# One stage of a two-layer backbone: its instructions recorded, then issued in the order of a list scheduler in the kernel

## The chip, the cores and the metric

The kernel runs on one core of one Trainium2 chip. The metric is the device time of one execution in microseconds (us), lower is better. The core's engines each run their own queue in order: TensorE (PE, with its weight loads shown apart as PEld), VectorE (DVE), ScalarE (ACT), GpSimd (POOL) and SyncE (SP, which here only issues DMAs). POOL's queue issues DMAs too.

## The reference

Two layers over 256 context tokens and 512 latent tokens of width 1024. What matters here is the RWKV-7 time mixing of layer 0, with 8 heads of 64 in both directions (d = 0 and 1), and the modulation vectors of all layers:

```python
def step(S, inp):
    r_t, w_t, k_t, v_t, a_t, b_t = inp
    sa = jnp.einsum('bhij,bhj->bhi', S, a_t)
    S = (S * w_t[:, :, None, :] + sa[..., None] * b_t[:, :, None, :]
         + v_t[..., None] * k_t[:, :, None, :])
    return S, jnp.einsum('bhij,bhj->bhi', S, r_t)
s_fin, ys = lax.scan(step, state0, xs, reverse=reverse)
...
def ada_mods(cvec, w, b):
    m = jax.nn.silu(cvec) @ w + b
```

After the scan come a norm per head, a bonus term and a gate (`rwkv_out`). Beside time mixing, layer 0 has latent attention (MLA); then an output projection, a mixture of experts, and layer 1 with grouped-query attention and its own mixture.

## The kernel before

The stages run one after the other: `front` (input projections), time mixing (`rwkv`, run from `program`), `mla`, `outproj`, `moe`, `gqa`, `outproj`, `moe`. The change touches time mixing.

**Time mixing.** The sequence is cut into 6 windows `w` of 128 tokens, each of two chunks `ci` of 64; both directions go through it together. Per window and direction `prep` makes decays and scaled keys (matmuls `psw`, `psa`, `psb`; tiles AR and BK). Per chunk `units` makes products of keys (`psB`, `psK`), transposes BK (`psT`) and writes the triangular matrix Ad to DRAM (`adr`). `tload` and `tinv` read it back in another layout (`Ts`), invert its 16x16 blocks on DVE and send them through DRAM again (`tdr`) to the tiles TP and TQ: four DMAs in a row that follow each other. `tmat` makes the whole inverse `T` from TP and TQ by a chain that goes to and fro between PE (`psG`, three `psX`) and DVE or ACT. `chain` carries the state: `cX`, `cU`, `cS` (the next state) and `cY` (the output). `rwout` is `rwkv_out` for one window; three of the six run inside the stage, the others in `mla`.

**Beside it** `ada_steps` makes the modulation vectors: 80 loads of 512 KB (`adaw`, from POOL, into two buffers), each with four matmuls into `psa`, then per 16 loads a sum on DVE (`adar`), four transposes (`pta`), a copy to `fm` and a DMA `rows<-adar`. The loads are issued two ahead, so load i+2 is asked for when the matmuls of load i are done.

**What sets the order.** Python generators merge the threads (`merge`). The Tile scheduler then issues everything in the order of its own simulated timeline, by priority. `urgent` raises the priority of `chain` (UC) and `tmat` (UT), and `tc.issue_after(last())` holds each group of `adaw` matmuls behind the last matmul of the chain traced so far (`K['at']`). All of `mla` is in the same scheduler.

Of the kernel before, what the change touches and what calls it, by code (L numbers as in the profile page):

```python
# [6 lines left out]
F32=mybir.dt.float32; F32R=mybir.dt.float32r; I32=mybir.dt.int32  # L7
AF=mybir.ActivationFunctionType; ALU=mybir.AluOpType
PSUM=bass.MemoryType.PSUM; DRAM=bass.MemoryType.DRAM
UC=2500; UT=2000; UE=3000; FI={9:(0,1),10:(3,)}; TL=((2,),(4,5))  # L10
CDEC=float(np.exp(np.float64(-0.5)))

def vw(ap, dims, off=0):

    return bass.AP(tensor=ap.tensor, offset=ap.offset+off, ap=[list(ap.ap[0])]+[list(d) for d in dims])

MAGIC=0x5f3759df
# [16 lines left out]
def rwkv(tc, nc, K, y, bon, sa):  # L34
# [29 lines left out]
    def prep(w,d):  # L64
        sp=sa; pre=U_.setdefault(w,[])
# [3 lines left out]
        r,k,kk=rkk[:,0],rkk[:,1],rkk[:,2]  # L69
        T4=lambda nm,tag=None: sp.tile([128,2,4,64],F32,tag=tag or nm,name=nm,bufs=1)  # L70

        sgw=sp.tile([128,2,4,65],F32,tag="sg",name="sg",bufs=1); sg=vw(sgw,[[261,2],[65,4],[1,64]]); nc.gpsimd.memset(vw(sgw,[[196,2],[65,4]],64),0.0)
        a=T4("a"); lora=((K['w2'],K['tw1'],K['w0h'],sg,d,big("psw")),(K['a2'],K['a1'],K['a0h'],a,1-d,big("psa")))
# [126 lines left out]
    def chain(w,ci):  # L200
# [5 lines left out]
        for d in range(2): mm(psX[:,d],lambda h,hp: pre[d][1][:,cs[d],h,hp,:],lambda h,hp: su[:,d,h,0,hp,:])  # L206
        K['at']=last[0]
        X=sp.tile([128,2,4,64],F32,name="X",bufs=1); nc.scalar.copy(X,psX)
        yield
        psU=chm("cU")  # L210
        for d in range(2): mm(psU[:,d],lambda h,hp: T[:,d,hp,h,:],lambda h,hp: X[:,d,hp,:])
        K['at']=last[0]
        for h,hs in enumerate(HS): nc.scalar.copy(su[hs,:,h,1],psU[hs])
# [14 lines left out]
        for h,hs in enumerate(HS):  # L228

            for i in range(8): d,hp=divmod(i,4); nc.tensor.matmul(psY[hs,d,hp,:],lhsT=su[hs,d,h,0,hp,:],rhs=pre[d][1][hs,cs[d],2,hp,:],start=i==0,stop=False,skip_group_check=True)  # L230
            for i in range(8): d,hp=divmod(i,4); hy=nc.tensor.matmul(psY[hs,d,hp,:],lhsT=su[:,d,h,1,hp,:],rhs=rb[:,d,h,hp,:],start=False,stop=True,skip_group_check=True)
            K['at']=hy.ins
        for d in range(2): addy(psY[:,d],win(w,d)*2+cs[d])
        if w+1<W: vload(w+1,ci)
        yield
    def steps(j):
        w,ci=divmod(j,2)
        u=units(w,ci)
        if ci==0:
# [43 lines left out]
    def then(*gs):  # L283
        for g in gs: yield from g
    def urgent(g,n):

        while True:
            with tc.high_priority(offset=n): x=next(g,g)
            if x is g: return
            yield  # L290
    def thread():
        N=2*W
        vload(0,0); vload(0,1)
        yield from merge(urgent(tmat(0,0),UT),steps(2))
        for j in range(N):
            g=[urgent(chain(*divmod(j,2)),UC)]
            if j+1<N: g.append(urgent(then(*([tinv(j//2+1)] if j%2 else []),tmat(*divmod(j+1,2))),UT))
            if j+3<N: g.append(steps(j+3))
            if j in FI: g.append(outs(FI[j],spare))
            yield from merge(*g[::-1])  # L300
# [1014 lines left out]
def program(tc,D,out):  # L1315
    nc=tc.nc
    with tc.tile_pool(reuse_waits="tile",name="g",bufs=1) as gp, tc.tile_pool(reuse_waits="tile",name="dr",bufs=1,space=DRAM) as dp:
# [13 lines left out]
        c=K.c; RW=[]; pd,dp2=pool("rwd",space=DRAM)  # L1331
        def early(psum):
# [4 lines left out]
            for o,n,m in ((0,'bones',128),(128,'hsel',32)): nc.vector.tensor_scalar(bo[:,o:o+m],c[n],1.0/64,None,op0=ALU.mult)  # L1337
            pa,sa=pool("rwa","right")
            ph=sa.tile([128,24],F32,name="ph")
# [74 lines left out]
```

## Time and profile before

| | |
|---|---|
| median of 3 runs | 1866.99 us (1865.08 to 1882.0) |
| the profiled execution's own time | 1878.29 us |
| its span, first to last instruction | 1876.6 us |
| mean granted TensorE clock (1.00 is 2.4 GHz) | 0.922 |
| busy: PE, DVE, ACT, POOL | 1600.1, 1252.2, 891.6, 481.5 us |
| time mixing, from 255 to 657 us of the span | 402 us: PE busy 312.0, DVE 226.9, ACT 133.8 |

Busy times are summed by the profiler from the instructions it saw; idle time is put down to the event that ended it (the releaser). An engine that is idle costs time only where it lies on the path to the end, so the stage is read by the waits on its busiest engine.

### The profile page before, as it was taken

The page shows a single profiled execution, that of the slowest core. Times are in us where ns is not written, and L with a number is a line of the kernel's source. Part 1 is how long each engine was busy: PE and PEld are TensorE (multiplying, and loading weights), DVE is VectorE, ACT ScalarE, POOL GpSimd, SP SyncE. Part 2 cuts the span into 40 slices and gives each one's busy share as a digit, 9 for nine tenths or more (in the row PEclk, how much of TensorE's full clock was granted, in tenths as well). Part 3 has the DMA queues.
Part 4 walks back from the last instruction along what each step waited for, and adds up shares of the span by engine and source line. Part 5 has one row for each costly group of instructions (what it writes and reads, how often), then busy time and mean ns, then how long its engine had stood idle before and what let it go on. Part 6 is the DMA issues. An engine that isn't in the chain of part 4 may idle for free.

```text
span 1876.6 us, 31790 instructions
## 1 busy us (share of the span) xinstructions
PE 1600.1 (85%) x12258; PEld 1225.2 (65%) x12258; DVE 1252.2 (67%) x2306; ACT 891.6 (48%) x1734; POOL 481.5 (26%) x512
## 2 busy tenths in 40 slices
PE   4999968777788787899986999969969999779986
PEld 2888856555576675566864877757746667457765
DVE  3575666555555586554487978777975553889986
ACT  5432644333332263665233867526356663447651
POOL 0222011111111032000244776063500001524324
PEclk8999879888789897899988999989989999889998
DMA  9245456676755220101646999752020004469974
GB/s 357 67 115 138 115 153 174 198 211 172 208 164 143 53 97 24 45 1 54 207 157 205 362 364 322 266 170 75 14 65 23 1 12 159 161 229 366 359 291 168
DMA packets 179002, 303.39 MB, mean 162 GB/s; under 512 B 93968, under 2 KB 107152, under 8 KB 177824
## 3 DMA queue, kind: packets, MB, share of 16 engines
q1 hardware_dynamic: 142576, 189.61, 30.3%
q0 software_dynamic: 29984, 101.27, 16.3%
q10 hardware_dynamic: 6288, 10.45, 1.8%
q8 instruction: 97, 1.59, 0.3%
q14 instruction: 57, 0.47, 0.1%
HBM read 266.99 MB, written 42.15 MB: 165 GB/s over the span
## 4 chain that ended last, share of the span: by engine, by line
PE 51%; DVE 18%; DMA 14%; issue 10%; ACT 4%; POOL 2%; SPq 1%; ACTq 0%; POOLq 0%; DVEq 0%
PE ps L959 7%; PE ps L510 6%; DMA adaw<-in_ada_w 6%; PE sc L650 4%; PE pt L664 4%; PE pv L672 4%; PE py L959 3%; PE py L836 3%; PE ps L836 3%; DMA w<-in_w_ex 3%; PE psq L595 3%; DVE wl L401 3%; PE ps L1240 1%; PE psX L42 1%; PE psa L452 1%
## 5 line engine op out<-in xcount | busy, mean ns | idle before, releaser
L401 DVE TENSOR_TENSOR wl<-w,wh 128x1024 fp32r<-128x1024 f32 (+2 forms) x214 | 281.5, 1338 | 64.8 <-ACT wh L400 53.2
L400 ACT CAST wh<-w 128x1024 fp32r<-128x1024 f32 (+2 forms) x241 | 246.9, 1048 | 131.1 <-PE ps L959 30.9
L959 PE MATMUL ps<-wh,xTl 128*128 128x512 f32 x336 | 136.9, 408 | 10.8 <-DVE xTl L401 9.4
L959 PE MATMUL ps<-wh,xTh 128*128 128x512 f32 x336 | 136.7, 407 | 3.9 <-ACT xTh L400 3.9
L959 PE MATMUL ps<-wl,xTh 128*128 128x512 f32 x336 | 133.7, 398 | 0.0
L651 DVE TENSOR_REDUCE nm<-sc 128x1 f32<-128x768 f32 (+1 forms) x112 | 96.5, 879 | 53.5 <-PE sc L650 52.7
L664 PE MATMUL pt<-cst,p 128*128 128x128 f32 x608 | 107.7, 291 | 11.3 <-ACT pT L666 6.5
L653 ACT ACTIVATE p<-sc,nm 128x768 f32<-128x768 f32 (+1 forms) x112 | 94.0, 842 | 44.6 <-DVE nm L651 44.6
L443 POOL DMA_DIRECT2D adaw<-in_ada_w x80 | 42.4, 532 | 274.2 <-PE psa L452 262.6
L664 PEld LDWEIGHTS pt<-cst,p 128*128 128x128 f32 x608 | 68.6, 143 | 56.5 <-issue 33.8
L672 PE MATMUL pv<-pT,vv 128*64 128x256 f32 x608 | 101.3, 413 | 1.1 <-ACT pT L666 0.6
L452 PE MATMUL psa<-adaw,sct 128*32 128x256 f32 x640 | 62.7, 459 | 40.2 <-DMA adaw<-in_ada_w 37.5
L1142 POOL DMA_INDIRECT w<-in_w_ex,wat x72 | 87.3, 1213 | 35.9 <-DVE wl L401 18.2
L401 POOL TENSOR_TENSOR wl<-w,wh 128x1024 fp32r<-128x1024 f32 x27 | 69.5, 2593 | 84.6 <-ACT wh L400 84.5
L510 PE MATMUL ps<-hhi,wh 128*128 128x512 f32 (+1 forms) x240 | 81.1, 346 | 5.0 <-DVE hhi L400 5.0
L959 PEld LDWEIGHTS ps<-wh,xTl 128*128 128x128 f32 x336 | 64.3, 191 | 29.5 <-DVE xTl L401 15.1
L510 PE MATMUL ps<-hlo,wh 128*128 128x512 f32 (+1 forms) x240 | 81.9, 342 | 0.0
L510 PE MATMUL ps<-hhi,wl 128*128 128x512 f32 (+1 forms) x240 | 81.8, 343 | 0.0
L666 ACT COPY pT<-pt 128x512 f32<-128x512 f32 x104 | 60.2, 586 | 44.5 <-PE pt L664 43.9
L959 PEld LDWEIGHTS ps<-wh,xTh 128*128 128x128 f32 x336 | 64.7, 193 | 17.1 <-ACT xTh L400 5.8
L401 DVE TENSOR_TENSOR xTl<-pt,xTh 128x512 fp32r<-128x512 f32 x84 | 55.8, 681 | 27.1 <-ACT xTh L400 26.1
L959 PEld LDWEIGHTS ps<-wl,xTh 128*128 128x128 f32 x336 | 64.6, 192 | 12.9
(611 smaller groups left out, 4321.0 us busy)
## 6 DMA issues: line engine op xcount, KB each, us to landing
w<-in_w_ex SPq DMA_DIRECT2D x120, 512.0 KB
adaw<-in_ada_w POOLq DMA_DIRECT2D x80, 512.0 KB
Yd<-yb SPq DMA_DIRECT2D x35, 512.0 KB
w<-in_w_sh SPq DMA_DIRECT2D x24, 512.0 KB
rkk<-rkk SPq DMA_DIRECT2D x12, 768.0 KB
adaw<-in_ada_w SPq DMA_DIRECT2D x8, 1024.0 KB
w<-in_w_rw SPq DMA_DIRECT2D x15, 512.0 KB
SU<-Vd SPq DMA_DIRECT2D x48, 128.0 KB
```

The costliest lines, as they stand in the source:

```text
L400: e1(hi,src)
L401: return e2(lo,src,hi.bitcast(F32),ALU.subtract)
L452: nc.tensor.matmul(ps[32*c:32*c+32,256*h:256*h+256],lhsT=K.sc[:,k,:],rhs=w[:,256*c:256*c+256],start=k+h==0,stop=k==7,skip_group_check=True ...
L510: nc.tensor.matmul(ps[:,:n],lhsT=a[:,k,:],rhs=b[:,k,sl],start=k+j==0,stop=k==7 and j==2)
L650: for m,(a,b) in enumerate(pl): nc.tensor.matmul(ps[:,c0:c0+cn],lhsT=a,rhs=b[:,c0:c0+cn],start=m==0,stop=m==len(pl)-1)
L651: nm=sp.tile([128,1],F32,name="nm",bufs=8); i1=nc.vector.tensor_reduce(nm,ps[:,:n],X,ALU.max,negate=True)
L653: K.late=i1,nc.scalar.activation(p[:,:n],ps[:,:n],AF.Exp,bias=nm,accum_out=rs[:,j:j+1])
L664: for j in range(nq): nc.tensor.transpose(pt[:,y,128*j:128*j+128],PR[y][0][j][:,128*kt:128*kt+128],K.ident)
L672: nc.tensor.matmul(po[64*y:64*y+64,:w],lhsT=v(h+y,kt),rhs=T[:,y],start=kt==0,stop=kt==nk-1,skip_group_check=True)
L836: nc.tensor.matmul(ps,lhsT=a[:,128*i:128*i+128],rhs=b[:,k%2,:],start=j==0,stop=j==23); j+=1
L959: for n,(x,y) in enumerate(((a[0],b[0]),(a[0],b[1]),(a[1],b[0]))): nc.tensor.matmul(ps,lhsT=x,rhs=y,start=first and n==0,stop=last and n==2)
L1142: return lambda t,j: nc.gpsimd.indirect_dma_start(out=t,out_offset=None,in_=D['w_ex'],in_offset=bass.IndirectOffsetOnAxis(ap=ix[:,j:j+1],a ...
```

## The change

`program` wraps the builder `nc` in a class `Plan`. Between `nc.start()` and `nc.stop()`, that is for all of time mixing's main part and `ada_steps`, instructions are recorded and not issued (`keep`), with the areas that they read and write and so what each depends on; tiles that take a buffer over depend on its former users. `stop` puts PE instructions of one kind and one merge step (`SEG`) into groups, prices every instruction from a table (`cost`; a DMA lands 2.2 us and its bytes' time after its issue, one DMA's bytes at a time, `wire`), finds for each group the longest way to the end (`bl`), and runs a list scheduler with those prices: a free engine takes the ready group with the longest way. The groups are then issued in that order in a `manual_schedule` block. The priorities (`urgent`) of the main part and `issue_after` for the `adaw` matmuls are gone, and a small memset in `prep` (`sg`) goes from POOL to DVE. No other instruction is added or taken away. `front`, with the first steps of time mixing, and `mla` are scheduled as before.

```diff
-UC=2500; UT=2000; UE=3000; FI={9:(0,1),10:(3,)}; TL=((2,),(4,5))
+UE=3000; FI={9:(0,1),10:(3,)}; TL=((2,),(4,5))
...
+    def cost(self,o):
+        e,n,m=o['eng'],o['n'],o['m']
+        if m=='dma_start': return 0.06 if e=='sync' else 1.0
+        if e=='tensor':
+            if m=='transpose': return 0.109 if n>=128 else 0.07
+            k=o['sh'][0]; c=0.072 if n<=64 else n*0.00168
+            if o['p']==32: return c*0.4
...
+        if e=='scalar': return 0.22+n*0.00076
+        return 0.9+n*0.002
+    def wire(self,o):
...
+        return b/(3.4e5 if row>=2048 else 2.4e5 if row>=1024 else 1e5)
...
+    def stop(self):
+        self.on=False; ops=self.ops; N=len(ops)
...
+        lat=[(2.2+self.wire(ops[g[0]])) if dma[k] else t[k]+(0.1 if eng[k]=='tensor' else 0)+SEM for k,g in enumerate(G)]
...
+        for k in reversed(order): bl[k]=lat[k]+max((bl[s] for s in succ[k]),default=0.0)
...
+            for e in self.ENG:
+                while free[e]<=now and ready[e]:
+                    _,k=heapq.heappop(ready[e]); done+=1; out.append(k); at[k]=now
+                    free[e]=now+t[k]; heapq.heappush(wake,free[e])
+                    if dma[k]:
+                        b=self.wire(ops[G[k][0]]); dfree=max(dfree,now)+b; end=dfree+2.2
+                    else: end=now+lat[k]
+                    heapq.heappush(fut,(end,k))
...
+        with self.tc.manual_schedule():
+            for k in out:
+                for i in G[k]: o=ops[i]; o['f'](*o['a'],**o['k'])
...
-nc.gpsimd.memset(vw(sgw,[[196,2],[65,4]],64),0.0)
+nc.vector.memset(vw(sgw,[[196,2],[65,4]],64),0.0)
...
-            g=[urgent(chain(*divmod(j,2)),UC)]
-            if j+1<N: g.append(urgent(then(*([tinv(j//2+1)] if j%2 else []),tmat(*divmod(j+1,2))),UT))
+            g=[chain(*divmod(j,2))]
+            if j+1<N: g.append(then(*([tinv(j//2+1)] if j%2 else []),tmat(*divmod(j+1,2))))
...
+    nc=Plan(tc,tc.nc)
...
-            main,tail=body(sp,pp)
-            run_all(merge((ada_steps(nc,tc,K,[(0,1),(0,2),(1,0),(1,1),(1,2)],D,sp,pp,lambda: Q.get('at')),1),(main,PM)))
+            sp,pp=nc.pool(sp),nc.pool(pp); main,tail=body(sp,pp); nc.start()
+            run_all(merge((ada_steps(nc,tc,K,[(0,1),(0,2),(1,0),(1,1),(1,2)],D,sp,pp,lambda: None),1),(main,PM)))
+            nc.stop()
```

The order moves on every engine. In the rows below, L172 is the line of the change that issues the recorded instructions, L26 the wrapper's line for all others; `x4` counts equal instructions.

**Place 1: PE, early in the stage.** Before, from the first direction matmuls of a `prep` to the state matmuls of the first chunk:

```order
L75 MATMUL psw<-tw_96,w_98 128x128 x4
L452 MATMUL psa<-adaw,sct 32x256 x4
L75 MATMUL psa<-a_97,a_99 128x128 x4
L42 MATMUL cU<-X,T_2314 64x64
L452 MATMUL psa<-adaw,sct 32x256 x4
L42 MATMUL cU<-X,T_2314 64x64 x15
L42 MATMUL psG<-TQ_1578,Aoff 64x64 x16
L452 MATMUL psa<-adaw,sct 32x256 x4
```

The change, PE, from the end of a `prep`'s matmuls past the `cX` of the second chunk:

```order
L172 MATMUL psw<-tw_96,w_98 128x128
L172 MATMUL psa<-a_97,a_99 128x128
L172 MATMUL cX<-SU,AR_1622 64x64 x8
L172 MATMUL cX<-SU,AR_1807 64x64 x8
L172 MATMUL psa<-adaw,sct 32x256 x4
L172 MATMUL psX<-Aoff,L_2313 64x64 x16
L172 MATMUL psa<-adaw,sct 32x256 x4
L172 MATMUL psb<-q,hs 32x128 x4
```

Matmuls of one kind are no longer cut into, `psw` and `psa` of a `prep` always alternate, and loads of `adaw` are spread over the whole stage.

**Place 2: DVE, from the end of a `tinv` (`Ts<-tmp`) to the transpose that needs what came back through DRAM (TP and TQ).** Before, third window:

```order
L170 TENSOR_REDUCE Ts_1913<-tmp_2254 128x8x8
L467 TENSOR_SCALAR A_8910<-fm_85 128x16
L468 TENSOR_TENSOR A_8910<-A_8910,par 128x16
L108 TENSOR_TENSOR bon<-psb,bon 128x128
L124 TENSOR_TENSOR AR_1807<-psB,cst 64x256
L125 TENSOR_TENSOR Rb_2368<-psB,cst 128x256
L124 TENSOR_TENSOR AR_1807<-psK,cst 64x256
L125 TENSOR_TENSOR Rb_2368<-psK,cst 128x256
L184 STREAM_TRANSPOSE TP_1568<-TQ_1576 128x256
```

The change, the same window:

```order
L172 TENSOR_TENSOR kd<-kd,rkk 128x512
L172 TENSOR_TENSOR BK_1808<-bb,En 128x8x64
L172 SCALAR_TENSOR_TENSOR AR_1807<-rkk,E_2521 64x2x256 x2
L172 TENSOR_TENSOR AR_1807<-rkk,E_2521 128x2x256
L172 TENSOR_TENSOR BK_1808<-kd,En 128x8x64
L172 TENSOR_TENSOR q<-rkk,kd 128x512
L172 TENSOR_TENSOR Aoff<-Ad_1669,cst 128x512 x2
L172 TENSOR_TENSOR SU<-cS,Dw 64x256 x2
L172 TENSOR_TENSOR AR_1807<-psB,cst 64x256
L172 TENSOR_TENSOR Rb_2330<-psB,cst 128x256
L172 TENSOR_TENSOR AR_1807<-psK,cst 64x256
L172 TENSOR_TENSOR Rb_2330<-psK,cst 128x256
```

Right ahead of these rows stands `Ts<-tmp`, right behind them `bon<-psb,bon` and the transpose: the instructions of a whole `prep` now stand in the time of the way through DRAM.

**Place 3: PE and SP, the end of the stage.** PE before, from the last `cU` on; `ro`, `pt` and `pq` belong to `mla`:

```order
L42 MATMUL cU<-X,T_2315 64x64 x15
L231 MATMUL cY<-Rb_2581,SU 64x64 x8
L230 MATMUL cY<-AR_2764,SU 64x64 x4
L230 MATMUL cY<-AR_3109,SU 64x64 x4
L231 MATMUL cY<-Rb_2581,SU 64x64 x8
L256 MATMUL ro<-y,bo_1522 128x512
L736 MATMUL pt<-cst,p 128x128 x5
```

PE in the change, the same place:

```order
L172 MATMUL cU<-X,T_2315 64x64 x16
L172 MATMUL psa<-adaw,sct 32x256 x4
L172 MATMUL rg<-sgw,roc 128x128 x4
L172 MATMUL psa<-adaw,sct 32x256 x4
L172 MATMUL cY<-Rb_2366,SU 64x64 x16
L172 MATMUL psa<-adaw,sct 32x256 x40
L172 MATMUL pta<-cst,adar 128x128 x4
L26 MATMUL ro<-y,bo_1522 128x512
L26 MATMUL pt<-cst,p 128x128 x5
```

SP in the change, its last rows of the stage and the first loads of `mla` (before, the last `rows<-adar` stood 17 rows ahead of `p<-pm`):

```order
L26 DMA rov<-vD 128x4x128
L26 DMA sgw<-sgd 128x128
L172 DMA rows<-adar 128x512
L26 DMA p<-pm 128x672
L26 DMA wraw<-in_wq 128x768 x2
L26 DMA mg<-in_mg 128x256
L26 DMA rp<-in_ropem 128x256
```

The matmuls of the last 10 of the 80 `adaw` loads moved behind the last `cY`, and `mla`'s first loads and matmuls stand behind them. On ACT the last copy `fm<-pta`, and on DVE the last sum `adar`, stand ahead of `mla`'s first instructions in the same way.

## Rows read from the trace of the kernel before

**Rows 1.** Busy times by stretch: us, PE, PEld, DVE, ACT, POOL, PE clock, DMA share, GB/s

```profile
255.00:657.00 402.00, 311.96 (x5210) 245.30 (x5208) 226.85 (x515) 133.80 (x333) 46.92 (x92) 0.85 0.60 167
605.00:657.00 52.00, 40.63 (x649) 35.69 (x648) 27.44 (x59) 13.37 (x27) 3.84 (x4) 0.87 0.23 60
100.00:150.00 50.00, 50.00 (x282) 43.19 (x281) 37.11 (x24) 16.76 (x27) 13.08 (x18) 1.00 0.51 132
400.00:450.00 50.00, 36.21 (x573) 27.14 (x571) 19.62 (x42) 15.02 (x39) 6.05 (x13) 0.80 0.68 196
```

**Rows 2.** Waits of PE from 255 to 657: total us, times, longest

```profile
PE psa L452 <- DMA adaw<-in_ada_w: 37.5, 27, 4.1
PE psG L42 <- DMA TQ<-tdr: 17.5, 4, 8.5
PE psX L42 <- DVE Aoff L195: 10.1, 5, 5.8
PE cU L42 <- DVE T L198: 7.8, 10, 2.4
PE cX L42 <- DMA SU<-Vd: 6.2, 3, 3.6
```

**Rows 3.** Chain that ended last, five stretches: start, us, piece

```profile
254.73 4.05 DMA adaw<-in_ada_w
...
285.26 4.29 DMA adaw<-in_ada_w
...
290.56 4.80 DMA adaw<-in_ada_w
...
402.69 9.19 DMA tdr<-Ts
...
463.23 3.81 DMA adaw<-in_ada_w
...
475.57 8.52 DMA adaw<-in_ada_w
...
607.71 2.75 DMA tdr<-Ts
...
614.43 2.50 DMA TQ<-tdr
```

**Rows 4.** Timeline of PE at 288, 304 and 316 us: start, us, what

```profile
288.19 1.11 PE L75 MATMUL psw<-tw,w 64*128 64x128 f32 x8
...
304.20 1.07 PE L452 MATMUL psa<-adaw,sct 128*32 128x256 f32 x16
...
316.10 0.27 PE L75 MATMUL psa<-a,a 64*128 64x128 f32 x1
316.10 0.27 PE L75 MATMUL psw<-tw,w 64*128 64x128 f32 x1
316.21 0.27 PE L75 MATMUL psa<-a,a 64*128 64x128 f32 x1
```

**Rows 5.** Waits of DVE from 255 to 657

```profile
DVE TP L184 <- DMA TQ<-tdr: 27.6, 8, 11.9
DVE y L59 <- PE cY L231: 26.3, 5, 8.5
DVE Ts L152 <- DMA Ts<-adr: 24.6, 5, 8.7
```

**Rows 6.** Timeline of DVE in the third window

```profile
401.33 0.68 DVE L170 TENSOR_REDUCE Ts<-tmp 128x64 f32<-128x512 f32 x1
...
408.82 0.41 DVE L125 TENSOR_TENSOR Rb<-psK,cst 128x256 f32<-128x256 f32 x1
415.06 0.45 DVE L184 STREAM_TRANSPOSE TP<-TQ 128x256 f32<-128x256 f32 x1 [5.84 <-DMA TQ<-tdr]
```

**Rows 7.** Timeline of SP and of PE where the stage ends

```profile
652.32 0.32 SPq L711 DMA_DIRECT2D p<-pm  x1
656.62 0.81 SPq L717 DMA_DIRECT2D wraw<-in_wq  x2
...
655.40 1.15 PE L231 MATMUL cY<-Rb,SU 128*64 128x64 f32 x16
...
658.35 0.71 PE L736 MATMUL pt<-cst,p 128*128 128x128 f32 x5
...
661.36 0.62 PE L747 MATMUL pq<-wqh,qah 128*128 128x384 f32 x2 [0.94 <-ACT qah L739]
```

More of the change, by code (lines that the diff above doesn't have):

```diff
@@ L8 @@
 AF=mybir.ActivationFunctionType; ALU=mybir.AluOpType
-PSUM=bass.MemoryType.PSUM; DRAM=bass.MemoryType.DRAM
-UC=2500; UT=2000; UE=3000; FI={9:(0,1),10:(3,)}; TL=((2,),(4,5))
+PSUM=bass.MemoryType.PSUM; DRAM=bass.MemoryType.DRAM; SEG=[0]
+UE=3000; FI={9:(0,1),10:(3,)}; TL=((2,),(4,5))
 CDEC=float(np.exp(np.float64(-0.5)))
@@ L70, in prep @@
         T4=lambda nm,tag=None: sp.tile([128,2,4,64],F32,tag=tag or nm,name=nm,bufs=1)
-        sgw=sp.tile([128,2,4,65],F32,tag="sg",name="sg",bufs=1); sg=vw(sgw,[[261,2],[65,4],[1,64]]); nc.gpsimd.memset(vw(sgw,[[196,2],[65,4]],64),0.0)
+        sgw=sp.tile([128,2,4,65],F32,tag="sg",name="sg",bufs=1); sg=vw(sgw,[[261,2],[65,4],[1,64]]); nc.vector.memset(vw(sgw,[[196,2],[65,4]],64),0.0)
         a=T4("a"); lora=((K['w2'],K['tw1'],K['w0h'],sg,d,big("psw")),(K['a2'],K['a1'],K['a0h'],a,1-d,big("psa")))
@@ L206, in chain @@
         for d in range(2): mm(psX[:,d],lambda h,hp: pre[d][1][:,cs[d],h,hp,:],lambda h,hp: su[:,d,h,0,hp,:])
-        K['at']=last[0]
         X=sp.tile([128,2,4,64],F32,name="X",bufs=1); nc.scalar.copy(X,psX)
@@ L211, in chain @@
         for d in range(2): mm(psU[:,d],lambda h,hp: T[:,d,hp,h,:],lambda h,hp: X[:,d,hp,:])
-        K['at']=last[0]
         for h,hs in enumerate(HS): nc.scalar.copy(su[hs,:,h,1],psU[hs])
@@ L231, in chain @@
             for i in range(8): d,hp=divmod(i,4); hy=nc.tensor.matmul(psY[hs,d,hp,:],lhsT=su[:,d,h,1,hp,:],rhs=rb[:,d,h,hp,:],start=False,stop=True,skip_group_check=True)
-            K['at']=hy.ins
         for d in range(2): addy(psY[:,d],win(w,d)*2+cs[d])
@@ L293, in thread @@
         vload(0,0); vload(0,1)
-        yield from merge(urgent(tmat(0,0),UT),steps(2))
+        yield from merge(tmat(0,0),steps(2))
         for j in range(N):
-            g=[urgent(chain(*divmod(j,2)),UC)]
-            if j+1<N: g.append(urgent(then(*([tinv(j//2+1)] if j%2 else []),tmat(*divmod(j+1,2))),UT))
+            g=[chain(*divmod(j,2))]
+            if j+1<N: g.append(then(*([tinv(j//2+1)] if j%2 else []),tmat(*divmod(j+1,2))))
             if j+3<N: g.append(steps(j+3))
@@ L324, in merge @@
         t=min(live,key=lambda x: x[2])
+        SEG[0]+=1
         try: next(t[0]); t[2]+=1.0/t[1]
@@ L1315, in program @@
 def program(tc,D,out):
-    nc=tc.nc
+    nc=Plan(tc,tc.nc)
     with tc.tile_pool(reuse_waits="tile",name="g",bufs=1) as gp, tc.tile_pool(reuse_waits="tile",name="dr",bufs=1,space=DRAM) as dp:
@@ L1330, in program @@
         p4,g4=pool("g4"); tw1=g4.tile([128,768],F32,name="tw1"); a1=g4.tile([128,768],F32,name="a1"); w2=g4.tile([128,512],F32,name="w2"); a2=g4.tile([128,512],F32,name="a2")
-        c=K.c; RW=[]; pd,dp2=pool("rwd",space=DRAM)
+        c=K.c; RW=[]; pd,dp2=pool("rwd",space=DRAM); dp2=nc.pool(dp2)
         def early(psum):
@@ L1337, in early @@
             for o,n,m in ((0,'bones',128),(128,'hsel',32)): nc.vector.tensor_scalar(bo[:,o:o+m],c[n],1.0/64,None,op0=ALU.mult)
-            pa,sa=pool("rwa","right")
+            pa,sa=pool("rwa","right"); sa=nc.pool(sa)
             ph=sa.tile([128,24],F32,name="ph")
```

127 lines of the change are left out of this document (added).

## The prediction

> **What bounds the kernel now.** I read the busy times by stretch first, to see what the changed stage is made of. Time mixing's main part takes 402 us [rows 1], a fifth of the span. PE is its busiest engine with 312 us, DVE has 227 and ACT 134. So PE idles for 90 us, and the chip grants PE a mean clock of 0.85 there, where a stretch with no gap in PE's work, 100 to 150 us, has 1.00 and one with 14 us of gaps in 50 has 0.80 [rows 1]. A matmul at the lower level, 1.2 GHz, takes twice its time at 2.4, so the stage loses twice by its gaps: the gap itself, and slower matmuls.
>
> How much work is there for PE? A mean of 0.85 between two levels means that 30% of the time was at 1.2 GHz. With the stage's own busy share (312/402) that puts 312 x 0.85 = 265 us of work at full clock into it. That is the floor if nothing else binds; the other engines are below it.
>
> Next the waits of PE, to see what fills the 90 us. The largest is the wait for an `adaw` load, 37.5 us in 27 places [rows 2]. It is no work of time mixing: PE's queue is in order, and a matmul of `ada_steps` that stands at its head before its load has landed holds up everything behind. `psG` waits 17.5 us for TQ, that is for the way through DRAM, and 8.5 of it are one wait, at the start of the stage. The rest, `psX`, `cU`, `cX` and smaller ones, makes 35 us: the to and fro with DVE and ACT. DVE itself waits 27.6 us for TQ and 24.6 for `Ts` [rows 5], both from DRAM, and holds up what stands behind in its own queue.
>
> **The change part by part.** Instructions stay the same, so the sum has four terms: work of PE, its idle time, its clock, and what stands at the end.
>
> *PE's work.* From 265 us come off two things. In three of the nine `prep`s of the stage `psw` and `psa` stood apart, four and four, as in place 1; eight passes of `psw` alone took 1.11 us [rows 4], and where the two alternated, as in the other six, a pass of each started every 0.11 us, 0.9 us for all sixteen. So 3 x 1.1 = 3 us. And the matmuls of 10 of the 80 loads go behind the stage (below): 16 passes, two loads, took 1.07 us [rows 4], so 10 x 0.53 = 5 us. It leaves 257 us.
>
> *Waits for `adaw`.* A load takes 3.81 to 8.52 us from its issue to its use [rows 3], mostly 4 to 5; I take 4.8. With two buffers the matmuls of load i need at least that much other work on PE since those of load i-2. I added up the matmuls that stand between in the two orders, priced as the rows price them at full clock, and summed what is missing to 4.8 us at each load: 91 us before, where loads stand close (place 1 has three within 3 us), and 25 us in the main part of the change. The trace shows 37.5 us of idle for the 91 [rows 2]; in the same proportion 25 gives 10. The gain is 27 us. Its ends are 0 (everything runs faster, so loads must land faster too) and 37.5.
>
> Here the Trainium skill has a price of its own. Its page "DMA: Bandwidth & Descriptors", section "Anatomy of one DMA — SWDGE (gpsimd) path", fits a DMA issued by GpSimd as 2.0 us plus its bytes at 436 KB per us; for 512 KB that is 3.2 us (an estimate from that page). The trace disagrees: no load that ended a wait took under 3.81 us [rows 3]. By the page the tail computed below would take 4 us less and the result would be 1830.
>
> *The way through DRAM.* From the end of `tinv` to the transpose that needs what came back, the order before leaves DVE seven small instructions, which cover little: the reduce at 401.33 was followed by a transpose at 415.06, with 5.84 us of plain idle just before it [rows 6], while `tdr` took 9.19 us to land; in a quieter stretch `tdr` took 2.75 and TQ 2.50 [rows 3]. In the change (place 2) a whole `prep` stands there, some 16 instructions of 0.4 to 0.7 us, 9 us in all. So of DVE's 27.6 us I expect most to go, but PE had only 17.5 - 8.5 = 9 us of idle from it inside the stage, and I count 5 us. Ends: 0 and 9. For the remaining 35 us I see no reason for a change on the whole: the list scheduler puts a group of other matmuls between one `psX` and the next, but every place of its order assumes prices, and a DMA of 64 KB at 2.2 us plus 0.65 us is below what loaded stretches show (9.19 [rows 3]).
>
> Idle time: 90 - 27 - 5 = 58 us. The new order is worth what its table is worth; so the ends are 30 us, when it holds, and 115, when late DMAs move every engine's head against the others.
>
> *The clock.* With fewer gaps I take 0.90, between the stage's own 0.85 and 1.00 [rows 1]. Work takes 257 / 0.90 = 286 us, with ends 302 and 257. The main part: 286 + 58 = 344 us, against 402: 58 us less.
>
> *The memset* moved from POOL to DVE is nine times about 0.1 us on an engine that is 56% busy, and POOL is freed of it; I count nothing. If DVE were the bound it would cost 1 us.
>
> *The tail.* This is the change's own cost. Behind the last `cY` stand 40 matmuls for 10 loads (place 3), and the buffers allow two loads at a time. One has landed by then, one was asked for about 2 us before (only `cY<-Rb` stands between), and eight come in four pairs, of which each can be asked for only when the matmuls before it are done. A quiet load takes 4.05 to 4.80 us [rows 3], the matmuls of one 0.53, those of the pair's second up to that again: about 5 us a pair, 20 us, with the first two 22.5. Other engines have nothing to fill this with: on PE, DVE, ACT and SP the last steps of `ada_steps` stand ahead of `mla`'s first ones. Then `adar` (0.7), the issue of `rows`, and only then `p<-pm`, which before went out at 652.32, ahead of the last `cY`, and so cost nothing. I count 0.6 for the issue, 3.5 for a landing that no row shows by itself (between 2.50 and 4.80 [rows 3]), and then the 3.0 us from `pt` at 658.35 to `pq` at 661.36 [rows 7]. So `pq` starts 30 us after the last `cY`, against 4.8 before (that one ends at 656.55 [rows 7]). The tail costs 25 us, with ends 18 (3.81 us a load, a short landing) and 33.
>
> **The sum.** -58 + 25 = -33 us. The profiled execution took 1878.3 us, so it would take 1845. It is 11 us above the median of the runs, 1867.0, for a reason that the stage doesn't show; I take the difference off the median: 1834 us.
>
> **The rivals.** *Full engines (14%).* The table holds, DVE's stalls are covered, PE idles 30 us and gets a clock of 0.97: 257 / 0.97 + 30 = 295, so -107 + 22 = -85: 1782 us. For it: the sum of PE's work is well above DVE's 227 us, and 100 to 150 us shows that PE can run without a gap. Against it: DMAs land at 2.5 to 9.2 us, and a fixed order can suit only one of these.
>
> *The tail eats it (20%).* The main part gains only what the spread of the loads gives and little clock: 90 - 15 = 75 us idle, 257 / 0.86 = 299, so 374: -28 + 25 = -3, 1864 us. For it: three quarters of the 90 us are waits that a rearranged order must meet again in some form. Against it: the clock follows the gaps.
>
> *Late DMAs in a fixed order (18%), slower.* The place is the four DMAs in a row from `adr` to TQ, once a window, five times in the stage. The order expects each some 2.9 us after its issue. If each lands at 8 to 9 us, as `tdr` did once at 9.19, and DVE's and PE's heads wait it out because what stands ahead of the transposes has run dry, that is 5 x 4 x 5.5 = 110 us, less the 45 us of work that place 2 puts there: 65 us on top of the 58. Main part 302 + 123 = 425: +23 + 30 = +53, 1920 us. It decides once idle time passes some 100 us, at the clock of before; then the tail is not paid for. For it: DMA engines are already busy 60% of the stage's time [rows 1], and a shorter stage packs them closer. Against it: before, the same four DMAs had less cover and cost PE 9 us inside the stage.
>
> *The order doesn't reach the engines:* had the Tile scheduler rearranged the block, the time would be that of another schedule. The built order rules it out, as place 1 shows unbroken groups; no chance is given.
>
> **How the numbers follow.** My forecast, 1834 us, gets 48%, as far as 1800 to 1850. The range has to take in most of the two cases beside it and part of the slow one: 1785 to 1890. A measurement of this kernel can tell 1%, 19 us, from no change. Faster by more than that (below 1848): the 14%, nearly all of my forecast's 48 and some luck of the third case, 0.63. Within 1%: 0.19. Slower (above 1886): 0.18, of which only the worse part lies outside the range.
>
> **What would show it.** Right: waits of PE for `adaw` under 15 us in the main part; DVE's waits for TQ under 10 us; PE's clock near 0.90; a stretch of 20 to 25 us behind the last `cY` in which PE only runs four matmuls every few us, waits for `adaw`, and DVE and ACT stand still; `pq` some 30 us behind the last `cY`. Wrong: PE idle over 75 us before the last `cY`, with `psG`, `psX` or `cU` the longest waits; or loads in the tail that land faster than any row of before. The forecast falls above all with the idle time of the main part, which no row of before can show for an order that it did not run.

## The result, and the profile after

The change took 1820.4 us (median of 4 runs, 1809.5 to 1820.9) against 1870.4 for the kernel before on the same chip: a ratio of 0.971 with a 95% interval of 0.965 to 0.977. It is faster by 50 us where I had forecast 33. The profiled execution has a span of 1819.2 us against 1876.6.

The stretches first, as in [rows 1]: the main part of time mixing (it now ends at 568.7 us, before at 656.6), the tail to `pq`, and the projections behind. Columns: us, PE, PEld, DVE, ACT, POOL, PE clock, DMA share, GB/s.

```profile
255.00:568.70 313.70, 262.54 (x5151) 211.66 (x5150) 224.38 (x530) 135.43 (x343) 44.92 (x79) 0.91 0.72 199
568.70:602.00 33.30, 15.94 (x95) 4.82 (x94) 3.17 (x9) 2.23 (x6) 4.24 (x8) 0.56 0.65 211
602.00:645.50 43.50, 40.81 (x232) 34.29 (x231) 40.40 (x128) 29.27 (x81) 19.60 (x35) 0.99 0.23 74
```

The main part lost 88 us: PE's busy time fell by 49, its idle time from 90 to 51, and its clock rose from 0.85 to 0.91. The tail gave 28 back (33.1 us from the last `cY` to `pq`, against 4.8). What waits are left in the main part, PE first, as in [rows 2]:

```profile
PE psa L172 <- DMA adaw<-in_ada_w: 14.0, 10, 3.1
PE cU L172 <- DVE T L172: 6.9, 8, 2.6
PE psG L172 <- DMA TQ<-tdr: 6.2, 2, 6.1
PE cX L172 <- DMA SU<-Vd: 6.1, 1, 6.1
PE psX L172 <- ACT L L172: 4.5, 3, 2.6
PE psG L172 <- DVE TQ L172: 4.3, 1, 4.3
PE psX L172 <- DVE Aoff L172: 3.4, 3, 1.5
```

The wait for `adaw` shrank from 37.5 us to 14.0 and the two of `psG` from 18.0 (17.5 for TQ's DMA) to 10.5. DVE's waits from 255 to 570 us, as in [rows 5]:

```profile
DVE TQ L172 <- DMA TP<-tdr: 14.7, 4, 6.7
DVE AR L172 <- ACT Ad L172: 14.2, 9, 6.2
...
DVE Ts L172 <- DMA Ts<-adr: 5.4, 2, 3.8
...
DVE TP L172 <- DMA TQ<-tdr: 2.4, 3, 1.2
```

The one for `Ts` fell from 24.6 to 5.4. The two waits for a piece from `tdr` cost 14.7 and 2.4 us, where the larger alone cost 27.6. The longest one stands in the second window. The third window is the one of [rows 6] and of place 2: there the transpose behind the reduce at 378.22 starts at 389.67 with no wait, where it had waited 5.84 us. Both in DVE's timeline:

```profile
334.98 0.45 DVE L172 STREAM_TRANSPOSE TQ<-TP 128x256 f32<-128x256 f32 x1 [6.72 <-DMA TP<-tdr]
...
378.22 0.68 DVE L172 TENSOR_REDUCE Ts<-tmp 128x64 f32<-128x512 f32 x1
...
389.67 0.43 DVE L172 STREAM_TRANSPOSE TQ<-TP 128x256 f32<-128x256 f32 x1
```

The tail, in the timeline of PE (where [rows 7] had the `pq` 4.8 us behind the last `cY`): start, us, what, and in brackets the idle time before.

```profile
566.81 1.90 PE L172 MATMUL cY<-Rb,SU 128*64 128x64 f32 x32
569.24 0.64 PE L172 MATMUL psa<-adaw,sct 128*32 128x256 f32 x8 [0.53 <-DMA adaw<-in_ada_w]
572.60 1.08 PE L172 MATMUL psa<-adaw,sct 128*32 128x256 f32 x8 [2.72 <-DMA adaw<-in_ada_w]
575.20 1.08 PE L172 MATMUL psa<-adaw,sct 128*32 128x256 f32 x8 [1.52 <-DMA adaw<-in_ada_w]
577.66 1.08 PE L172 MATMUL psa<-adaw,sct 128*32 128x256 f32 x8 [1.38 <-DMA adaw<-in_ada_w]
...
592.73 1.08 PE L172 MATMUL psa<-adaw,sct 128*32 128x256 f32 x8 [1.41 <-DMA adaw<-in_ada_w]
594.63 1.11 PE L172 MATMUL pta<-cst,adar 128*128 128x128 f32 x4 [0.81 <-DVE adar L172]
599.63 1.33 PE L26 MATMUL pt<-cst,p 128*128 128x128 f32 x5 [1.54 <-DMA p<-pm]
601.84 1.43 PE L26 MATMUL pq<-wqh,qah 128*128 128x384 f32 x2
```

Ten loads come, one every 2.5 us, a pair in 5.0 (five of the rows are left out). The trace shows each of a load's four matmuls as two passes; from the second load on, eight passes take 1.08 us, where the eight of the first, right behind the main part, took 0.64. The other engines have next to nothing to do (DVE is busy for 3.2 us of the 33, ACT for 2.2). DVE and SP in their timelines:

```profile
593.88 0.69 DVE L172 TENSOR_TENSOR adar<-psa,adar 128x512 f32<-128x512 f32 x1 [21.29 <-PE psa L172]
```

```profile
594.60 0.33 SPq L172 DMA_DIRECT2D rows<-adar  x1
595.29 0.32 SPq L26 DMA_DIRECT2D p<-pm  x1
```

### The profile page after: what moved, and what is told of

The parts are those of the page before. It is cut to its first block, busy times and chain, and to the rows that moved or that the text cites. A ratio compares the mean times of both kernels' runs of the same rounds, so it can differ in the third digit from the quotient of the medians.

```text
span 1819.2 us, 31808 instructions
## 1 busy us (share of the span) xinstructions
PE 1565.8 (86%) x12258; PEld 1194.1 (66%) x12258; DVE 1249.9 (69%) x2318; ACT 891.5 (49%) x1734; POOL 482.9 (27%) x500
## 5 line engine op out<-in xcount | busy, mean ns | idle before, releaser
L26 DVE TENSOR_TENSOR wl<-w,wh 128x1024 fp32r<-128x1024 f32 (+2 forms) x214 | 280.6, 1334 | 70.7 <-ACT wh L26 60.3
L26 ACT CAST wh<-w 128x1024 fp32r<-128x1024 f32 (+2 forms) x241 | 246.5, 1048 | 135.8 <-PE ps L26 65.1
L26 PE MATMUL ps<-wh,xTl 128*128 128x512 f32 x336 | 137.9, 410 | 10.5 <-DVE xTl L26 8.9
L26 PE MATMUL ps<-wh,xTh 128*128 128x512 f32 x336 | 137.5, 409 | 6.0 <-ACT xTh L26 3.9
L26 PE MATMUL ps<-wl,xTh 128*128 128x512 f32 x336 | 134.5, 400 | 0.0
L26 DVE TENSOR_REDUCE nm<-sc 128x1 f32<-128x768 f32 (+1 forms) x112 | 96.4, 879 | 54.7 <-PE sc L26 53.9
L26 PE MATMUL pt<-cst,p 128*128 128x128 f32 x638 | 113.1, 291 | 11.6 <-ACT pT L26 4.8
L172 POOL DMA_DIRECT2D adaw<-in_ada_w x80 | 42.5, 532 | 275.4 <-PE psa L172 259.9
L26 ACT ACTIVATE p<-sc,nm 128x768 f32<-128x768 f32 (+1 forms) x112 | 94.0, 842 | 43.6 <-DVE nm L26 43.5
L26 PEld LDWEIGHTS pt<-cst,p 128*128 128x128 f32 x638 | 73.0, 144 | 58.3 <-issue 33.4
L26 POOL DMA_INDIRECT w<-in_w_ex,wat x72 | 90.0, 1250 | 43.7 <-DVE wl L26 25.8
L26 PE MATMUL pv<-pT,vv 128*64 128x256 f32 x608 | 100.6, 411 | 1.1 <-ACT pT L26 0.6
L26 POOL TENSOR_TENSOR wl<-w,wh 128x1024 fp32r<-128x1024 f32 x27 | 70.1, 2613 | 82.7 <-ACT wh L26 82.7
L26 PE MATMUL ps<-hhi,wh 128*128 128x512 f32 (+1 forms) x240 | 81.2, 346 | 5.0 <-DVE hhi L26 5.0
L26 PEld LDWEIGHTS ps<-wh,xTl 128*128 128x128 f32 x336 | 64.7, 193 | 29.8 <-DVE xTl L26 14.9
L26 PE MATMUL ps<-hlo,wh 128*128 128x512 f32 (+1 forms) x240 | 82.9, 346 | 0.0
L26 ACT COPY pT<-pt 128x512 f32<-128x512 f32 x104 | 60.2, 586 | 46.1 <-PE pt L26 45.4
L26 PE MATMUL ps<-hhi,wl 128*128 128x512 f32 (+1 forms) x240 | 82.7, 346 | 0.0
L172 PE MATMUL psa<-adaw,sct 128*32 128x256 f32 x640 | 57.5, 437 | 28.9 <-DMA adaw<-in_ada_w 28.8
L26 PEld LDWEIGHTS ps<-wh,xTh 128*128 128x128 f32 x336 | 65.2, 194 | 19.6 <-ACT xTh L26 5.8
L26 DVE TENSOR_TENSOR xTl<-pt,xTh 128x512 fp32r<-128x512 f32 x84 | 55.8, 682 | 27.9 <-ACT xTh L26 27.7
L26 PEld LDWEIGHTS ps<-wl,xTh 128*128 128x128 f32 x336 | 65.1, 194 | 13.2
```

The source lines that it names most:

```text
L26: if not self.plan.on: return f(*a,**k)
L172: for i in G[k]: o=ops[i]; o['f'](*o['a'],**o['k'])
```

## The experiments

Two questions were open. Which property of the new order made the main part shorter by 88 us? And what sets the end of the stage, if the tail is taken away? My theory: the order by the longest way covers the waits, and the tail is a cost of its own that can be had back. The rivals: the hold that the change dropped, or the grouping of equal matmuls, made the gain; and loads that are moved out of the tail cost the same elsewhere. Each ratio is to the kernel before on the same chip; the chips differ between some of the runs, so that two runs are better compared by their ratios than by their times.

**Run 1: only the hold on the loads' matmuls dropped.**

```diff
 # the kernel before
-  run_all(merge((ada_steps(...,lambda: Q.get('at')),1),(main,PM)))
+  run_all(merge((ada_steps(...,lambda: None),1),(main,PM)))
```

> The kernel before with one thing of the change alone: the adaw matmuls no longer held behind the chain's last matmul (issue_after gone for them). My theory, that the gain comes from covered waits, from matmuls of one kind left together and from the clock that follows, needs the new order: 1845 to 1875 us, and PE's waits for adaw inside the stage stay above 25 us. The rival, that the chain's hold on the adaw matmuls was the whole loss, expects 1815 to 1835 us with those waits under 15 us.

Measured: 1871.6 us, ratio 1.001 (0.998 to 1.004). That is the first theory's range, with 38.2 us of PE's waits for `adaw` left in the stage. The last `cY` starts at 647.2 instead of 656.3 us, but nothing of these 9 us arrives at the end. So the hold is not what the change gained by; in the stage it can be 9 of the 88 us at most.

**Run 2: recorded and grouped as in the change, but issued in the order recorded.**

```diff
-            for k in out:
+            for k in range(len(G)):
```

> The changed kernel, recorded and grouped as it is, but the groups are issued in the order in which the program traced them; prices and longest way decide nothing. My theory expects at least 30 us more than the change, 1850 us or above, with DVE's waits for TQ and Ts back over 40 us in sum. The rival, that recording and grouping in a manual block is what helps, expects the change's time within 10 us, 1810 to 1830.

Measured: 2066.8 us, ratio 1.106 (1.100 to 1.112). The last `cY` starts at 849.2 us. PE's waits from 255 to 849 us are led by these two, for DVE and not for DMAs (DVE itself waits 122.5 us for `Ts` from DRAM, above the 40 expected for TQ and `Ts` together):

```profile
PE psb L172 <- DVE q L172: 103.8, 9, 13.2
PE psG L172 <- DVE Aoff L172: 74.8, 5, 21.4
```

So recording and grouping alone loses 195 us, and the computed order wins all of that and 50 more. That the computed order makes the gain is shown. That it has to be the order by the longest way is not: a list scheduler that takes the ready groups by another rule was not tried.

**Run 3: ten of the loads left out.**

```diff
+    todo=[t for i,t in enumerate(todo) if not 68<=i<78]
```

> The changed kernel without 10 of the last 16 adaw loads and their matmuls (part of the modulation of layer 1 is left out). My theory of the tail expects that nothing is left behind the last cY but one or two loads, and the time falls by 22 to 30 us against the change, to 1790 to 1798. The rival, that the tail hides work of the next stage which would have waited anyway, expects 8 us or less, 1812 or above.

Measured: 1780.4 us, ratio 0.952 (0.945 to 0.959), 40 us below the change by the medians and 35 by the ratios, more than the 22 to 30 that I expected. `pq` starts at 570.2 us instead of 601.8, the last `cY` at 561.1 instead of 568.5: 24 us come from the tail, which is 9 us long instead of 33, and 7 from the main part. But this run also takes the bytes and matmuls of ten loads away (part of the modulation vectors is not computed), so it does not tell whether another place would be cheaper.

**Run 4: the loads halved, in four buffers instead of two.**

```diff
-    todo=[... for k in range(8) for h in range(2)]
+    todo=[... for k in range(8) for h in range(4)]
-        w=sp.tile([128,1024],F32,name="adaw",bufs=2); ...
+        w=sp.tile([128,512],F32,name="adaw",bufs=4); ...
```

> The changed kernel with the adaw loads cut in two: 160 of 256 KB into four buffers of half the size, the same memory; each has two matmuls. In the order 12 loads (of half the size) stand behind the last cY instead of 10. My theory expects the tail to fall from 25 us to some 14 us (three rounds of four loads at 3.5 us and four times 0.3 us of matmuls) and the main part to stay: 1805 to 1814 us. The rival, that twice as many DMAs crowd POOL and the DMA engines, expects the main part longer by over 10 us: 1822 or above.

Measured: 1811.4 us, ratio 0.968 (0.963 to 0.973). `pq` starts 19 us behind the last `cY` instead of 33, but the main part is 7 us longer. It is 9 us below the change, at the edge of what I can tell. The halving has a price on PE. Its stretch up to the last `cY`, and one half load in its timeline:

```profile
255.00:575.90 320.90, 287.16 (x5157) 216.14 (x5158) 222.94 (x520) 132.46 (x333) 85.29 (x157) 0.94 0.73 200
```

```profile
561.40 0.63 PE L172 MATMUL psa<-adaw,sct 128*32 128x256 f32 x4
```

The four passes of a half load took 0.63 us, as long as the eight of a whole one (0.64). In the code the four matmuls of a whole load go to four column blocks of the array (`tile_position`), the two of a half load to two. So PE is busy for 287 us up to the last `cY` instead of 262; its rows of `adaw` alone are busy for 78.7 us instead of 47.1.

**Runs 5 to 7: prices and groups.** The measured table replaced by two numbers; the landing time of a DMA raised; the groups cut to four.

```diff
 # run 5, in cost(), after the DMAs
+        return 0.07 if e=='tensor' else 0.5
 # run 6, in lat= and in end=
-  2.2+self.wire(...)
+  4.2+self.wire(...)
 # run 7
-  len(G[last[1]])<32
+  len(G[last[1]])<4
```

> The change with its table of measured times replaced by two numbers: 0.07 us for every instruction of TensorE and 0.5 us for every other (the planner's prices of DMAs stay). If the measured times do the work, the main part of the stage loses what it gained where engines other than TensorE wait on one another: the last cY comes later than in the change (568.7 us from the start) by 15 us or more, and with about one load instead of ten behind it the time is 1815 to 1850 us. If only the rule of the longest way counts, the last cY comes at 570 to 590 us, since the loads that now lie ahead of it bring about 10 us of work with them, the tail behind it is under 12 us instead of 33, and the time is 1795 to 1815 us, below the change's 1820.

> The change with the planner's landing time of a DMA raised from 2.2 to 4.2 us, near the 4.3 to 5.1 us that the trace of the change shows for the 64 KB pieces of Ts, SU and TQ. If the waits left in the main part (51 us idle on TensorE) come from DMAs that land later than planned, the waits of VectorE for the TQ and TP pieces (17 us) and of TensorE for SU and TQ (12 us) fall by half, and the last cY comes some 10 to 15 us before 568.7; against it stand six more loads behind the last cY (16 instead of 10), at 2.5 us each, so that the time is 1820 to 1825 us. If the late DMAs cost nothing that another wait does not take over, the last cY moves only by the six loads' own work (6 us) and the time is 1828 to 1840 us.

> The change with groups of at most 4 instructions instead of 32, so that the order changes from one kind of matmul to another more often. Three loads instead of ten stand behind the last cY, so the tail should be 15 us instead of 33. If unbroken rows of equal matmuls are why TensorE's work in the stage came out lower than forecast, its busy sum in the main part rises by 8 us or more over the change's 262.5 and most of the shorter tail is lost: 1815 to 1835 us. If rows do not matter, the busy sum grows only by the seven loads' own matmuls (about 6 us), the last cY comes at 570 to 580 us, and the time is 1800 to 1812 us.

Measured: 1819.4 us (ratio 0.973, 0.970 to 0.977), 1831.3 (0.980, 0.976 to 0.983) and 1833.8 (0.982, 0.979 to 0.986).

Run 5 met its first theory, that the measured times do the work, in both numbers: the last `cY` starts at 603.4 us, 35 later than in the change, and the time is 1819. But all loads lie ahead of that `cY`, and `pq` follows after 7 us. Run 8 below, which keeps the measured times and also has all loads ahead, has its last `cY` at 604.1. So the late `cY` goes with the place of the loads and does not speak for the table: with all loads ahead, the two prices and the whole table did equally well. It is a comparison of two runs only; they differ in the plan's single wire too, and both keep the planner's prices of DMAs.

Run 6 moved the last `cY` to 556.8 us, with six loads more behind it. That is 12 us earlier; by run 8's rate below (3.6 us a load) six loads less explain 21. DVE's waits for TQ and TP fell from 17.1 us to 3.6, as the first theory wanted, but PE's for SU and TQ did not (13.4 against 12.3), and the time lies in the second theory's range. The nearer price brought nothing here.

Run 7 confirmed its first theory. PE's busy time up to the last `cY` rose to 290.1 us, 28 more than in the change, of which the seven loads more that lie ahead explain about 4 (0.57 each). Its stretch up to the last `cY`:

```profile
255.00:585.10 330.10, 290.06 (x5181) 223.02 (x5182) 222.64 (x513) 131.46 (x332) 44.87 (x81) 0.92 0.74 200
```

Two of PE's groups from 255 us to `pq`, first in the change, then in run 7 (columns: busy us, mean ns of one, idle time before):

```profile
L172 PE MATMUL psX<-Aoff,L 128*64 128x64 f32 x768 | 29.1, 230 | 4.4 <-DVE Aoff L172 3.4 <-issue 0.9
...
L172 PE MATMUL psG<-TQ,Aoff 128*64 128x64 f32 x384 | 15.7, 240 | 10.5 <-DMA TQ<-tdr 6.2 <-DVE TQ L172 4.3
```

```profile
L172 PE MATMUL psX<-Aoff,L 128*64 128x64 f32 x768 | 41.7, 228 | 0.1
...
L172 PE MATMUL psG<-TQ,Aoff 128*64 128x64 f32 x384 | 22.7, 244 | 15.5 <-DMA TQ<-tdr 11.2 <-DVE AR L172 3.0 <-DVE Aoff L172 0.8
```

One matmul of `psX` takes the same 228 to 230 ns in both, and 768 of them keep PE busy for far less than 768 times that: in a row each starts before the one ahead has ended. The 41.7 us against 29.1 are not all lost, since a group's busy time also counts the time in which matmuls of another group run beside it. Counted from each start to the next, at the clock granted at that moment, `psX` took 26 us in the change and 30 in run 7, and a matmul of another kind followed one of `psX` 27 and 122 times. Most groups rose by 1 to 4 us like this one; what broken rows cost in all is the 24 us by which PE is busy longer.

**Runs 8 to 10: no load left behind.** The plan lets all transfers pass one after the other through a single wire. That keeps the loads back, so that ten stand behind the last `cY`. Without it none does. Run 9 adds the halved loads of run 4, run 10 also the 4.2 us of run 6 (in `lat=`).

```diff
-  b=self.wire(ops[G[k][0]]); dfree=max(dfree,now)+b; end=dfree+2.2
+  end=now+lat[k]
```

> The change with one line of its planner altered: a transfer lands 2.2 us and its own wire time after its issue, whatever else is under way, where the change lets all transfers pass one after the other through a single wire, which the plan keeps busy for 253 of its 283 us. In the order that comes out no adaw load stands behind the last cY (10 in the change). If the single wire is what left the loads to the end, and the chip carries them earlier at once, the last cY comes at 575 to 582 us (568.7 plus the ten loads' own matmuls, 0.64 us each, and their weight loads), pq 5 to 9 us behind it, and the time is 1800 to 1810 us. If the chip's transfers are as short of room as the plan said (199 GB/s in the main part of the change, 206 GB/s in its tail), the loads end late all the same: TensorE's waits for adaw in the main part rise from 14 us to over 30, pq stays near 600 us and the time is 1815 to 1830 us.

> The same planner line altered, and the adaw loads in four buffers of 256 KB as in the earlier experiment with small loads, which left six of them behind the last cY; none is left now. If the tail in that experiment (18 us from the last cY to pq) came from the plan's single wire, pq comes 9 to 12 us earlier than there (595.0), at 583 to 586 us, and the time is 1798 to 1803 us, the shortest so far with the whole computation. If the four buffers were already as fast as the chip carries, the last cY moves back by as much as the tail shrinks and the time stays at 1808 to 1815 us.

> As the run before, and the landing time of a transfer in the plan raised from 2.2 to 4.2 us. No load stands behind the last cY here either, so that the price alone is tried, without the longer tail that it brought before. If a nearer price spares waits (there the last cY came at about 557 us with six loads fewer ahead of it, which is 5 us less than their own work explains), TensorE's waits for TQ, SU and T fall by 5 us or more and the time is 4 to 8 us below the run before. If it only trades one wait for another, the two are within 4 us of each other.

Measured: 1823.8 us (ratio 0.975, 0.971 to 0.978), 1822.6 (0.974, 0.968 to 0.979) and 1801.2 (0.962, 0.958 to 0.965).

Run 8 refuted my theory of the tail. The tail is gone, and the main part is longer by 35.6 us: the last `cY` starts at 604.1. Its stretch and the first of PE's waits in it:

```profile
255.00:604.10 349.10, 278.49 (x5200) 218.10 (x5196) 222.15 (x518) 132.52 (x333) 45.12 (x83) 0.87 0.70 193
```

```profile
PE psa L172 <- DMA adaw<-in_ada_w: 42.2, 31, 4.5
```

PE waits 28 us more for loads than in the change's main part, and its clock is 0.87 against 0.91. A load that is moved from the tail into the main part costs 3.6 us there, of which 0.6 is its matmuls. Run 9 has its last `cY` at the same time: it waits less for loads (26.7 us), but PE is busy longer with the halved ones (288 us against 278). Run 10 is 21 us below run 9 and has the lowest ratio with all loads in the stage. Of the 21 us, 8 lie ahead of the first score of attention (table below); the others lie behind it, where both run the same instructions. The waits for TQ and SU did not fall, as the first theory has it: `psG` waits 25.2 us for TQ where run 9 has 6.3, and the waits for `adaw` are 10.2 where run 9's are 26.7 (all from 255 to 585 us). With run 6, which brought nothing, I can't say more of the landing time than that the stage was 8 us shorter in this order.

**Runs 11 and 12: one group of loads out of the stage.** 16 of the 80 loads are merged into the projections behind, 11 in the change, 12 in run 10.

```diff
-  ada_steps(nc,tc,K,[(0,1),(0,2),(1,0),(1,1),(1,2)],...)
+  ada_steps(nc,tc,K,[(0,1),(0,2),(1,0),(1,1)],...)
-  pq=pp("pq",3)
+  pq=pp("pq",2)
-  run_all(merge(tail(room),tiles()))
+  run_all(merge(merge(tail(room),tiles()),
+                ada_steps(nc,tc,K,[(1,2)],D,su,pp_,lambda: None)))
```

> The change, whose planner and table stay as they are, with the loads of one of the five groups (16 of 80) taken out of the stage and merged into the projections that follow it, where the DMA engines are busy 0.06 to 0.24 of the time; pq goes from three PSUM buffers to two, which makes room for psa there. Nothing of the computation is left out. If the stage is bound by what the loads bring through the DMA engines, it ends earlier by as much as with 10 loads left out or more: the last cY at 560 us or before and pq 5 us behind it, so that pq starts some 35 us earlier than in the change; the projections pay 10 to 17 us for 16 loads of 0.64 to 1.08 us on TensorE, and the time is 1792 to 1805 us. If the loads only end up waiting elsewhere (the projections are longer by the 40 us that 16 loads take at 2.5 us each), nothing is won: 1815 to 1830 us.

> The same 16 loads (here 32 of 256 KB) moved into the projections, on top of the fastest version so far (four buffers of 256 KB, no single wire in the plan, a landing time of 4.2 us; 1801 us). If the two edits work on different things, pq comes 20 us or more before that version's 601.9 us and the time is 1780 to 1795 us. If both do no more than take the loads off the end of the stage, they do not add up, and the time is that of the other run of this call within 5 us.

Measured: 1793.3 us (ratio 0.964, 0.959 to 0.968) and 1791.3 (0.962, 0.958 to 0.967); the kernel before took 1861.1 on this chip, so that the ratios are to be compared, not the times. Run 11 is 31 us below the change by its span (1788.4), but only 14 by the ratios, whose intervals overlap. Its main part, and its projections from `pq` to the first score of attention:

```profile
255.00:549.50 294.50, 254.94 (x5061) 206.20 (x5062) 220.26 (x515) 132.50 (x331) 37.91 (x68) 0.92 0.72 196
558.20:642.90 84.70, 70.77 (x448) 51.74 (x448) 70.06 (x202) 42.06 (x112) 38.73 (x63) 0.90 0.45 142
```

`pq` starts 43.6 us earlier than in the change, and the projections take 84.7 us instead of 73.4: 16 loads that cost the stage some 44 us cost 11 there, and the first score comes 32 us earlier than in the change. So the loads did not end up waiting elsewhere in the profiled executions; how much of the 32 us arrives at the end, between 14 and 31, is open. Run 12's time met both of its theories, so it decides nothing by itself. The stage says that the two edits do not add up: the last `cY` is 19 us behind run 11's, with PE busy for 269 us instead of 255, and the ratio is run 10's.

Side by side, from the profiled executions: how many of 80 loads (whole ones) lie ahead of the last `cY`, where it starts, where `pq` and the first score of attention start, the span, and PE's work up to the last `cY` as busy time x granted clock.

```
               loads   cY     pq     score   span    work
before          80    656.3  661.4  738.2  1876.6   265
1 no hold       80    647.2  652.2  727.3  1870.1   264
2 as recorded   80    849.2  854.0  930.9  2064.5   231
change          70    568.5  601.8  675.2  1819.2   239
3 ten left out  70    561.1  570.2  638.5  1779.9   239
4 four buffers  74    575.9  595.0  670.4  1809.0   270
5 flat prices   80    603.4  610.8  684.1  1818.1   242
6 landing 4.2   64    556.8  605.8  680.8  1832.2   238
7 groups of 4   77    585.1  599.0  674.1  1823.3   267
8 no wire       80    604.1  609.5  679.8  1820.5   242
9 and 4 buffers 80    604.1  610.1  678.2  1821.9   262
10 and 4.2      80    596.6  601.9  670.0  1807.5   269
11 moved        64    549.5  558.2  642.9  1788.4   235
12 10 and moved 64    568.4  574.3  654.4  1788.2   253
```

From the first score on, all kernels run the same instructions, and yet this rest takes between 1133.6 and 1151.4 us. I found no cause for it in the stage. So a difference of under 18 us between two of these spans need not come from the stage; what the stage did is read from the columns up to the first score.

## Why the prediction held, and where its sizes were off

**The direction and the two main mechanisms were right.** The main part shortened, the tail took part of it back, and the time lies in the range.

*PE's work* was the mis-sized term. I had 257 us at full clock, from 265. The trace gives 262.5 x 0.91 = 239: 18 us less. The `psw` and `psa` alternate in the preps as forecast; this, in the timeline of PE, answers to [rows 4]:

```profile
314.22 0.27 PE L172 MATMUL psw<-tw,w 64*128 64x128 f32 x1
314.23 0.27 PE L172 MATMUL psa<-a,a 64*128 64x128 f32 x1
314.33 0.27 PE L172 MATMUL psw<-tw,w 64*128 64x128 f32 x1
314.34 0.27 PE L172 MATMUL psa<-a,a 64*128 64x128 f32 x1
```

The product is an estimate, since the clock is a mean over busy and idle time. Taken matmul by matmul, with the clock granted at that moment, the same traces have 264 us before, 244 in the change, 269 in run 7 and 254 in run 2 (whose product, 231, is far too low: PE idles long there, at a low clock). So the work fell by 21 us and not by 8. Of the 21, 6 are the ten loads and 4 `psw` and `psa` ([rows 4] give 2 x 1.11 - 0.9 = 1.3 us for each of three preps, so 4, where I wrote 1.1 and 3). The other 11 are what I left out. They are spread over many groups, `cY` with 5 and `psT` with 3 ahead. I put them down to rows that the order before broke up and that stand together now, but this is argued: run 7 shows that breaking the rows of the new order costs 25 us of work (4 of them for its seven loads), not that the order before lost by the same. The rows of `cX`, for one, were cut into 54 times before and 15 times in the change and took 13 us both times. The runs with halved loads have 253 to 270 for another reason, the price of the halving in run 4.

*The waits for `adaw`* are 14.0 us where I had 10, inside my sign of 15. *The way through DRAM*: my sign for DVE, under 10 us for TQ, was wrong. In DVE's queue 17.1 are left (14.7 + 2.4), and PE's idle time for `psG` is 10.5, near the 12.5 that I had kept (17.5 - 5). I had counted on a `prep` as cover. In the third window it stood there and there was no wait for TQ; in the second most of a `prep` stood there too, until 328 us, and DVE waited 6.72 us all the same.

*The other idle time*: I kept 35 us and found 51 - 14.0 - 10.5 = 27. *The clock*: 0.90 forecast, 0.91 found. The whole main part is 239 / 0.91 + 51 = 314 us against 344: 24 of the 30 come from PE's busy time, 7 from idle time.

*The tail* took 33.1 us against 30 forecast: pairs in 5.0 as worked out, ten loads and not 22.5 us of them but 24.6 (569.2 to 593.8), and 8 from there to `pq`. From the end of one load's matmuls (572.60 + 1.08) to the start of those of the load that takes its buffer (577.66) it is 4.0 us.

The Trainium skill's page "DMA: Bandwidth & Descriptors", section "Anatomy of one DMA — SWDGE (gpsimd) path", gives 3.2 us for such a load (an estimate by its fit). The trace of the tail does not agree: it has 4.0 with the issue. But the other buffer's load is under way at the same time there, so this is no test of the fit for one load alone.

*The sum*: -88 + 28 = -60 by the stage, -57 by the span and -50 between the medians, where I had -33. The main part gave 30 us more than forecast, 24 of them by PE's busy time; the tail took 3 more. Of the 10 us between the stage and the medians 8 are no loss: the profiled execution of the kernel before (1878.3 us) lay that much above its median.

**The rivals.** Full engines needed idle 30 and a clock of 0.97; the run has 51 and 0.91. (That rival also took 22 us for the tail where my own sum has 25, with no row for the difference.) The tail did not eat the gain. Late DMAs in a fixed order did not come about: they waited 1 to 7 us in a few places. The memset on DVE was not tried by itself; it shows as 0.07 us each time. The rival that I did not price was the one in my own sum: I treated the tail as a cost that stands apart from the main part. Runs 5, 8, 9 and 10 show that with all 80 loads in the stage `pq` comes at 602 to 611 us with a tail of under 8 us as well as at 602 with one of 33.

What stays open is what the loads are short of. The runs 5, 8, 9 and 10, with all 80 loads, move 191 to 198 GB/s up to the last `cY`, the change 199 and its tail 211, but run 11 moves 344 GB/s for 8 us; and 64 loads took 295 us in run 11 and 313 in run 12. Room on the DMA engines and the time of a round through the buffers were not told apart. A third buffer of full size was not tried.

## What to carry to other kernels

When an in-order engine waits for many small things, compute its order: here that was worth far more than the exactness of the prices, as two numbers for the engines' instructions did as well as the table. Keep equal matmuls in unbroken rows, and count what breaking them costs as work. Before a load is halved, look at how its matmuls share the array. And before a tail is filled, ask what the loads in it would push out: here they cost 2.5 to 3.6 us each wherever they stood in the stage, and 0.7 in the next one, where the DMA engines had been nearly idle.

## What the runs showed of the hardware

- Up to the last `cY`, PE was busy for 262 us with groups of up to 32 equal matmuls and for 290 with groups of up to 4 (the change and run 7), of which seven more loads explain 4; one 64-column matmul of `psX` took 228 to 230 ns in both.
- Four passes of a halved load (128x256, in two column blocks) took 0.63 us, the eight of a whole one (in four) 0.64.
- In the tail, with gaps of 1.4 us between groups of eight passes, the granted clock was 0.56, and eight passes took 1.08 us instead of 0.64. Behind it, the first two `pq` took 1.43 us together, and over the 43 us from 602 us on the clock was 0.99 again.
- 512 KB loads, two under way, came one every 2.5 us in the tail, with next to nothing else to load. In the main part the 64 KB pieces took 4.3 us (`adr` and `Ts`), 4.8 (TQ) and 2.6 (TP) to land (medians).
